# Holding one subtraction behind the last low part in the Fourier input folds of an encoder layer

## The chip, the cores and the metric

One core of a Trainium2 chip runs the whole layer as one program. The metric is the time of one execution on the device in microseconds (us). The five engines each take their own instructions in a fixed order: TensorE (PE: matmuls and transposes), VectorE (DVE), ScalarE (ACT), GpSimd (POOL) and SyncE (SP), which here issues nearly all transfers.

## The reference

The layer works on 256 tokens of width 2048 in float32. It is a feed-forward half-step, a pair of mixers, and a second feed-forward half-step. The change lies in the mixers:

```python
u = _rms_norm(h, pre_g)
q, k, v, f, g = jnp.split(u @ w_in, SPLIT_POINTS, axis=-1)
...
fg = f.astype(jnp.float32).reshape(b, s, FOURIER_GROUPS, FOURIER_GROUP_DIM)
mixed = jnp.real(jnp.fft.fft2(fg, axes=(1, 3), norm='ortho'))
...
gates = jax.nn.sigmoid((g.reshape(b, s, N_BRANCHES, D_MODEL) + b_gate).astype(jnp.float32)).astype(h.dtype)
merged = gates[:, :, 0] * y_attn + gates[:, :, 1] * y_four
```

The columns f (8 groups of 128 channels) go through a two-dimensional Fourier transform over tokens and over the channels of a group, of which the real part is kept. The columns q, k, v feed an attention, and g gives two gates.

## The kernel before, in words

**Split operands.** Every matmul operand is held as two float32r tiles, a high part and a low part: `split` (lines 101 and 102) lets ACT copy the source into the high part and then lets DVE subtract that from the source into the low part. A product is then three matmuls (`mm3`, lines 106 to 108): high by high, high by low, low by high. The function also remembers its last two instructions in `latest`; `latest["V"]` is the low part's subtraction on DVE.

**Weights.** A weight block of 512 columns and 2048 rows is walked by `col_block` in four groups `kg` of 512 rows. Each group comes in two pieces of 512 KB into `raw` tiles (5 buffers) and is split into `whi` and `wlo` tiles out of a ring of 6 slots. Each group costs PE 24 matmuls (4 row chunks, 2 token tiles, 3 products).

**Folds of f.** The weights of f are not multiplied as they are. The Fourier transform of real numbers has mirrored channels, so the host orders the columns of each of the 16 row chunks in pairs, and the kernel forms sums and differences of mirrored columns before it multiplies. For row chunk k, `load_f(k)` (line 615, with the helper `add_on_the_way` before it) issues a load of 512 KB from SP into a tile `fraw`, and then a second transfer from POOL's queue that adds the mirrored columns onto the front part on the way in, so that the front part holds sums (line 613). The tiles `fraw` live in the `chunk` pool, 6 slots in all (3 of each of two tags, used in turn), so the load of chunk k+6 takes the slot of chunk k.

`fold_f(k)` (line 622) then asks for the load of chunk k+4, and forms the differences in place on DVE (line 630: minus two times the back part, plus the sums). It splits the whole tile (`whi` on ACT, `wlo` on DVE), runs 12 matmuls into the two accumulators `pe`, and adds the sums, weighted by one scalar per row, into `zs` on DVE (line 643; line 641 for k = 0). That last instruction reads only the front part and one column pair behind it, which the subtraction doesn't write. The slot of `fraw` k is free when `wlo` of k, the last reader, is done.

**Where the folds stand.** Folds are called from inside four column blocks (the first block of q, and three of the gates) at row chunks 1, 5, 9 and 13, so one fold per group of weights: per fold the source has two raw pieces split, then one fold. Beside them lie the normalization and rotation of k and q (`norm_rope`, lines 535 to 558) and the gates (line 789).

**What sets the order.** The source order is not the order on the engines. A scheduler at build time orders each engine's instructions by when it thinks they are ready, within the dependencies it sees; on the chip each engine then keeps that order and waits at each instruction for what it needs. `tc.issue_after(ins)` adds an ordering without a wait: what is traced inside the block stands behind `ins` on `ins`'s engine. A stretch of DVE's order at the end of the first feed-forward step is written out by hand (`last_rows`), and instructions from outside may be put between its own.

Of the kernel before, what the change touches and what calls it, by code (L numbers as in the profile page):

```python
# [15 lines left out]
ALU = mybir.AluOpType  # L16
# [8 lines left out]
NB = 512  # L25
# [8 lines left out]
OW = GH * (HW - 1)  # L34
PO = 2 * (HW - 1)
NS = 2 * GH
EW = OW + NS
# [17 lines left out]
def encoder_layer(  # L55
# [23 lines left out]
    V, A, T = nc.vector, nc.scalar, nc.tensor  # L79
# [18 lines left out]
    latest = {}  # L98

    def split(hi, lo, src):  # L100
        a = A.activation(hi, src, AF.Copy)  # L101
        v = V.tensor_tensor(out=lo, in0=src, in1=hi.bitcast(F32), op=ALU.subtract)  # L102
        latest["A"], latest["V"] = a.ins, v.ins

    def mm3(ps, lh, ll, rh, rl, first, last):
        T.matmul(ps, lh, rh, start=first, stop=False)  # L106
        T.matmul(ps, lh, rl, start=False, stop=False)  # L107
        return T.matmul(ps, ll, rh, start=False, stop=last)  # L108
# [415 lines left out]
    for nm, g in (("q", gq), ("k", gk)):  # L524
        gc = const.tile([P, NT, HD], F32, name="gc" + nm)
        gs = const.tile([P, NT, HD], F32, name="gs" + nm)
        for t in range(NT):
            V.tensor_tensor(out=gc[:, t, :], in0=rc[:, t, :], in1=g[:], op=ALU.mult)
            v = lambda a: a.rearrange("p (a h c) -> p a h c", a=2, h=2)
            for half in range(2):  # L530
                V.tensor_tensor(out=v(gs[:, t, :])[:, :, half, :], in0=v(rsn[:, t, :])[:, :, half, :],
                                in1=v(g[:])[:, :, 1 - half, :], op=ALU.mult)
# [82 lines left out]
    def load_f(k):  # L615
        raw = chunk.tile([P, 2, NB], F32, tag=("ch_hi", "ch_lo")[k % 2], name="fraw")
        src = w_f[k].rearrange("p (b c) -> p b c", b=2)
        load(raw[:], src)
        add_on_the_way(raw[:, :, 0:OW], src[:, :, EW:NB])
        fraw[k] = raw  # L620

    def fold_f(k):

        if k == 0:
            pfold[0] = pmm.tile([P, NB], F32, tag="mm", name="pe")
            pfold[1] = ptr.tile([P, NB], F32, tag="tr", name="pe")
        if k + F_AHEAD < KD:
            load_f(k + F_AHEAD)
        raw = fraw.pop(k)
        V.scalar_tensor_tensor(out=raw[:, :, EW:NB], in0=raw[:, :, EW:NB], scalar=-2.0, in1=raw[:, :, 0:OW],  # L630
                               op0=ALU.mult, op1=ALU.add)
        hi = wring.tile([P, 2, NB], F32R, tag="hi", name="whi")
        lo = wring.tile([P, 2, NB], F32R, tag="lo", name="wlo")
        split(hi[:], lo[:], raw[:])
        e, o = slice(0, EW), slice(EW, NB)
        for b in range(2):
            mm = mm3(pfold[b][:, e], ueo[0][0][:, k, :], ueo[0][1][:, k, :], hi[:, b, e], lo[:, b, e], k == 0, False)
            with tc.issue_after(mm.ins):
                mm3(pfold[b][:, o], ueo[1][0][:, k, :], ueo[1][1][:, k, :], hi[:, b, o], lo[:, b, o], False, k == KD - 1)
        if k == 0:  # L640
            V.tensor_scalar(out=z2[:], in0=raw[:, :, e], scalar1=o0[:, k:k + 1], scalar2=None, op0=ALU.mult)
        else:
            V.scalar_tensor_tensor(out=z2[:], in0=raw[:, :, e], scalar=o0[:, k:k + 1], in1=z2[:],  # L643
                                   op0=ALU.mult, op1=ALU.add)
        if k == KD - 1:
            fs.extend(chunk.tile([P, 2, NB], F32R, tag="ch_" + c, name="f" + c[0]) for c in ("hi", "lo"))
            for b in range(2):
                split(fs[0][:, b, :], fs[1][:, b, :], pfold[b][:])
# [3 lines left out]
    def folds_at(n):  # L652

        now = [folds.pop(0) for _ in range(n)]
        return [(1 + i * KD // n, lambda k=k: fold_f(k)) for i, k in enumerate(now)]
# [389 lines left out]
```

## Time and profile before

| | us |
|---|---|
| median of 3 runs | 2133.01 (2130.24 to 2136.04) |
| the profiled execution, time | 2134.86 |
| its span in the profile | 2133.1 |
| PE busy | 2071.1 (97%) |
| DVE busy | 1317.3 (62%) |
| ACT busy | 1008.7 (47%) |
| POOL busy | 50.9 (2%) |

How to read it: the profiled execution's time is 1.8 us more than its span, and 1.9 us more than the median. A row of the waits says which engine and line waited for which, the total, the count and the longest. A row of a timeline begins with the start and the duration in us; a bracket at its end gives the idle time of the engine just before, and what ended it. SPq is SP issuing a transfer; the time to landing is not in that row. A row of the windows has the stretch and its length, the busy time and count of PE, PEld, DVE, ACT and POOL, the clock that PE was granted (1 is full), the DMA engines' share and GB/s. A row of a chain of waits has the start, the length and what the time was spent in.

### The profile page before, as it was taken

Reading aid. Unit: us, or ns where it says so; the run is one execution under the profiler, and the core shown is the slowest. Engines: PE = TensorE matmul, PEld = TensorE weight load, DVE = VectorE, ACT = ScalarE, POOL = GpSimd, SP = SyncE. Lnnn points to the kernel's source line nnn. Section 1 sums busy time; section 2 is a strip of 40 time slices with the busy share of each in tenths; the row PEclk is TensorE's granted clock in tenths of the full one; section 3 lists DMA queues with packets and bytes.
Section 4 is the critical chain, followed back from the end, with each engine's and each line's share of the span. In section 5 each row is a group of like instructions: output and inputs, shape, how many; then the busy total and the mean of one; then the engine's idle time right before and its main releaser. Section 6 shows DMA issues by size and latency. Waiting matters only on the chain.

```text
span 2133.1 us, 25216 instructions
## 1 busy us (share of the span) xinstructions
PE 2071.1 (97%) x9466; PEld 1713.9 (80%) x9466; DVE 1317.3 (62%) x1682; ACT 1008.7 (47%) x1336; POOL 50.9 (2%) x46
## 2 busy tenths in 40 slices
PE   9999999999999988779999999999999999999998
PEld 7888888888888867668888888878888888888886
DVE  6545555555555877546888887774455555555556
ACT  6444444444444546334676564554444444444443
POOL 0000000000000200000000000100000000000001
PEclk9999999999999999989999999999999999999999
DMA  8666555556566675554655657656555565555563
GB/s 316 209 219 191 190 189 192 193 190 191 186 194 195 211 241 174 159 157 134 194 183 188 198 174 246 209 170 207 195 189 190 186 197 193 191 189 188 192 194 108
DMA packets 117866, 411.10 MB, mean 193 GB/s; under 512 B 12872, under 2 KB 19024, under 8 KB 116336
## 3 DMA queue, kind: packets, MB, share of 16 engines
q1 hardware_dynamic: 113392, 405.36, 57.9%
q0 software_dynamic: 4352, 4.13, 1.3%
q8 instruction: 74, 1.21, 0.2%
q14 instruction: 48, 0.39, 0.0%
HBM read 405.25 MB, written 4.19 MB: 192 GB/s over the span
## 4 chain that ended last, share of the span: by engine, by line
PE 87%; DMA 6%; DVE 5%; issue 1%; ACT 1%; POOL 0%; SPq 0%; DVEq 0%; ACTq 0%; POOLq 0%
PE pc L107 17%; PE pc L108 17%; PE pc L106 17%; PE pr L108 10%; PE pr L107 10%; PE pr L106 10%; DMA fraw<-in_w_f 5%; DVE wlo L102 2%; PE pt L177 1%; DMA raw<-in_w_fo 1%; ACT whi L101 0%; DVE zs L643 0%; PE pt L760 0%; DVE h L390 0%; PE pf L108 0%
## 5 line engine op out<-in xcount | busy, mean ns | idle before, releaser
L102 DVE TENSOR_TENSOR wlo<-raw,whi 128x1024 fp32r<-128x1024 f32 (+1 forms) x711 | 866.8, 1222 | 672.1 <-ACT whi L101 670.6
L101 ACT ACTIVATE whi<-raw 128x1024 fp32r<-128x1024 f32 (+1 forms) x711 | 751.7, 1060 | 901.5 <-PE pc L108 534.9
L107 PE MATMUL pc<-wlo,uh 128*128 128x512 f32 x1840 | 720.9, 392 | 8.0 <-DVE wlo L102 8.0
L106 PE MATMUL pc<-whi,uh 128*128 128x512 f32 x1840 | 722.7, 393 | 5.5 <-ACT vt L846 3.4
L108 PE MATMUL pc<-whi,ul 128*128 128x512 f32 x1840 | 720.5, 392 | 1.9 <-DVE ul L102 1.9
L107 PEld LDWEIGHTS pc<-wlo,uh 128*128 128x128 f32 x1840 | 347.7, 189 | 81.0 <-DVE wlo L102 10.9
L106 PEld LDWEIGHTS pc<-whi,uh 128*128 128x128 f32 x1840 | 348.0, 189 | 78.1 <-ACT vt L846 3.8
L108 PEld LDWEIGHTS pc<-whi,ul 128*128 128x128 f32 x1840 | 347.8, 189 | 75.6 <-DVE ul L102 3.2
L106 PE MATMUL pr<-whi,hTh 128*128 128x512 f32 x688 | 269.4, 392 | 0.0
L108 PE MATMUL pr<-whi,hTl 128*128 128x512 f32 x688 | 267.8, 389 | 0.0
L107 PE MATMUL pr<-wlo,hTh 128*128 128x512 f32 x688 | 267.8, 389 | 0.0
L108 PEld LDWEIGHTS pr<-whi,hTl 128*128 128x128 f32 x688 | 129.1, 188 | 26.9
L107 PEld LDWEIGHTS pr<-wlo,hTh 128*128 128x128 f32 x688 | 129.2, 188 | 26.1
L106 PEld LDWEIGHTS pr<-whi,hTh 128*128 128x128 f32 x688 | 129.2, 188 | 26.1
L219 DVE TENSOR_TENSOR yf<-pr,yf 128x512 f32<-128x512 f32 (+1 forms) x82 | 55.1, 674 | 10.3 <-PE pr L108 9.7
L219 DVE TENSOR_TENSOR y<-pr,y 128x512 f32<-128x512 f32 x80 | 54.8, 686 | 4.1 <-PE pr L108 3.6
L106 PE MATMUL pr<-whi,oTh 128*128 128x512 f32 x128 | 50.3, 393 | 0.0
L108 PE MATMUL pr<-whi,oTl 128*128 128x512 f32 x128 | 50.0, 390 | 0.0
L107 PE MATMUL pr<-wlo,oTh 128*128 128x512 f32 x128 | 49.9, 390 | 0.0
L630 DVE SCALAR_TENSOR_TENSOR fraw<-fraw 128x504 f32<-128x504 f32 x16 | 10.9, 683 | 63.0 <-DMA fraw<-in_w_f 63.0
L106 PE MATMUL pr<-whi,mTh 128*128 128x512 f32 x120 | 46.9, 390 | 0.0
L108 PE MATMUL pr<-whi,mTl 128*128 128x512 f32 x120 | 46.7, 389 | 0.0
(300 smaller groups left out, 1416.7 us busy)
## 6 DMA issues: line engine op xcount, KB each, us to landing
raw<-in_f_up SPq DMA_DIRECT2D x176, 512.0 KB, 4.6
raw<-in_f_down SPq DMA_DIRECT2D x176, 512.0 KB, 4.5
raw<-in_f_gate SPq DMA_DIRECT2D x175, 512.0 KB, 4.3
raw<-in_w_in SPq DMA_DIRECT2D x112, 512.0 KB, 4.7
raw<-in_w_ao SPq DMA_DIRECT2D x32, 512.0 KB, 3.9
raw<-in_w_out SPq DMA_DIRECT2D x32, 512.0 KB, 4.5
fraw<-in_w_f SPq DMA_DIRECT2D x16, 512.0 KB, 4.5
raw<-in_w_fo SPq DMA_DIRECT2D x16, 512.0 KB, 4.4
```

What stands on the lines that cost most here:

```text
L101: a = A.activation(hi, src, AF.Copy)
L102: v = V.tensor_tensor(out=lo, in0=src, in1=hi.bitcast(F32), op=ALU.subtract)
L106: T.matmul(ps, lh, rh, start=first, stop=False)
L107: T.matmul(ps, lh, rl, start=False, stop=False)
L108: return T.matmul(ps, ll, rh, start=False, stop=last)
L177: T.transpose(pt[:, j, :], src[:, j * P:(j + 1) * P], ident[:])
L219: V.tensor_tensor(out=dst, in0=ps, in1=dst, op=ALU.add)
L630: V.scalar_tensor_tensor(out=raw[:, :, EW:NB], in0=raw[:, :, EW:NB], scalar=-2.0, in1=raw[:, :, 0:OW], op0=ALU.mult, op1=ALU.add)
```

## The change

The subtraction that forms the differences is put in a block that orders it behind `latest["V"]`, which at that place is the `wlo` of the second raw piece of the same group of weights. Nothing else in the source changes; the arithmetic is the same.

```diff
@@ fold_f(k)
         raw = fraw.pop(k)
-        V.scalar_tensor_tensor(out=raw[:, :, EW:NB], in0=raw[:, :, EW:NB], scalar=-2.0, in1=raw[:, :, 0:OW],
-                               op0=ALU.mult, op1=ALU.add)
+        with tc.issue_after(latest["V"]):
+            V.scalar_tensor_tensor(out=raw[:, :, EW:NB], in0=raw[:, :, EW:NB], scalar=-2.0, in1=raw[:, :, 0:OW],
+                                   op0=ALU.mult, op1=ALU.add)
         hi = wring.tile([P, 2, NB], F32R, tag="hi", name="whi")
         lo = wring.tile([P, 2, NB], F32R, tag="lo", name="wlo")
         split(hi[:], lo[:], raw[:])
```

In the changed file every line from 630 on stands one lower, so the subtraction is line 631 there and the accumulation of `zs` is line 644.

The first place is DVE at the end of the first feed-forward step, inside the stretch that is written by hand (`tot`, `pre`, `ca` to `cr` are steps of a root that scales the second token tile, `wlo<-raw` are low parts of weights, `fraw<-fraw` is the subtraction). Before:

```order
L376 TENSOR_REDUCE tot<-ssq_1997 128x1
L630 SCALAR_TENSOR_TENSOR fraw<-fraw 128x2x252
L378 TENSOR_SCALAR pre<-tot 128x1
L630 SCALAR_TENSOR_TENSOR fraw<-fraw 128x2x252
L156 SCALAR_TENSOR_TENSOR ca<-ssq_1997,pre 128x1
L630 SCALAR_TENSOR_TENSOR fraw<-fraw 128x2x252
L157 TENSOR_SCALAR ci<-ca 128x1
L102 TENSOR_TENSOR wlo<-raw,whi 128x1024
```

And with the change:

```order
L376 TENSOR_REDUCE tot<-ssq_1997 128x1
L378 TENSOR_SCALAR pre<-tot 128x1
L156 SCALAR_TENSOR_TENSOR ca<-ssq_1997,pre 128x1
L157 TENSOR_SCALAR ci<-ca 128x1
L102 TENSOR_TENSOR wlo<-raw,whi 128x1024
```

The subtractions of chunks 0 to 2 have left this stretch. Those of chunks 3, 4 and 5, which stood between low parts of weights in the block after it, have left that too; all six now stand among the folds.

The second place is DVE in the folds of the second column block, from the low part of chunk 2 to that of chunk 4 (`wlo<-fraw` is a fold's low part; `zs<-fraw` is the accumulation). Before, in the first two rows of `fraw<-fraw` and `zs` the chunk is 8, in the next two 9:

```order
L102 TENSOR_TENSOR wlo<-raw,whi 128x1024 x2
L630 SCALAR_TENSOR_TENSOR fraw<-fraw 128x2x252
L643 SCALAR_TENSOR_TENSOR zs<-fraw,o_5824,zs 128x520
L102 TENSOR_TENSOR wlo<-fraw,whi 128x1024
L102 TENSOR_TENSOR wlo<-raw,whi 128x1024 x2
L630 SCALAR_TENSOR_TENSOR fraw<-fraw 128x2x252
L643 SCALAR_TENSOR_TENSOR zs<-fraw,o_5824,zs 128x520
L102 TENSOR_TENSOR wlo<-fraw,whi 128x1024
```

With the change the rows of `fraw<-fraw` are chunks 2, 3 and 4, and those of `zs` chunks 7, 8 and 9:

```order
L631 SCALAR_TENSOR_TENSOR fraw<-fraw 128x2x252
L644 SCALAR_TENSOR_TENSOR zs<-fraw,o_5824,zs 128x520
L102 TENSOR_TENSOR wlo<-fraw,whi 128x1024
L102 TENSOR_TENSOR wlo<-raw,whi 128x1024 x2
L631 SCALAR_TENSOR_TENSOR fraw<-fraw 128x2x252
L102 TENSOR_TENSOR wlo<-fraw,whi 128x1024
L644 SCALAR_TENSOR_TENSOR zs<-fraw,o_5824,zs 128x520
L102 TENSOR_TENSOR wlo<-raw,whi 128x1024 x2
L631 SCALAR_TENSOR_TENSOR fraw<-fraw 128x2x252
L644 SCALAR_TENSOR_TENSOR zs<-fraw,o_5824,zs 128x520
L102 TENSOR_TENSOR wlo<-fraw,whi 128x1024
```

Before, the subtraction and the accumulation of one chunk stand together, and the low part behind them is that of a chunk five lower. Now the subtraction is that of the very chunk whose low part follows, and the accumulation has stayed where it was, five chunks ahead; it isn't ordered by the change. Counted over the folds, the accumulation of chunk k+5 stands ahead of the low part of chunk k for k = 1, 2, 4, 5, 6, 7, 9 and 10, and behind it for k = 3 and 8; before, the subtraction of chunk k+5 stood ahead of it for k = 1, 3, 4, 5, 6, 8, 9 and 10, and behind it for k = 2 and 7. SP's loads of chunks 6 to 15 keep their places between the pieces of weights, and POOL's order is the same.

## The prediction

> **What bounds the kernel now.** I read the page first, then PE's waits, the windows around them, the chain of waits there, and at last the rows of DVE.
>
> ```profile
> PE 2071.1 (97%) x9466; PEld 1713.9 (80%) x9466; DVE 1317.3 (62%) x1682; ACT 1008.7 (47%) x1336; POOL 50.9 (2%) x46
> L630 DVE SCALAR_TENSOR_TENSOR fraw<-fraw 128x504 f32<-128x504 f32 x16 | 10.9, 683 | 63.0 <-DMA fraw<-in_w_f 63.0
> PE pe L107 <- DVE wlo L102: 26.0, 8, 7.3
> PE pc L107 <- DVE wlo L102: 8.0, 5, 6.2
> PE pe L106 <- ACT q L546: 6.2, 1, 6.2
> PE pc L106 <- ACT vt L846: 3.4, 1, 3.4
> 820.00:860.00 40.00, 32.13 (x155) 26.88 (x154) 24.68 (x45) 18.51 (x31) 3.27 (x3) 0.91 0.57 159
> 957.40:964.30 6.90, 6.90 (x38) 5.93 (x37) 3.68 (x3) 4.25 (x6) 0.00 (x0) 1.00 0.57 178
> ```
>
> PE is busy for all but 62 us, and 44 of these are the four waits above. Behind them is DVE: the subtraction sits idle for 63 us in front of transfers into `fraw`. The folds run far below PE's pace: from 820 to 860 PE is busy 32 of 40 us at a clock of 0.91, while a window after the last subtraction is full, at a clock of 1. The chain of waits shows one turn of the folds, and DVE's rows (last two for SP) give ten such turns and their extremes:
>
> ```profile
> 858.59 3.53 DMA fraw<-in_w_f
> 862.79 5.15 DMA fraw<-in_w_f
> 868.63 0.76 DVE zs L643
> 869.38 1.15 DVE wlo L102
> 870.54 4.14 DMA fraw<-in_w_f
> 819.74 1.22 DVE L102 TENSOR_TENSOR wlo<-fraw,whi 128x1024 fp32r<-128x1024 f32 x1
> 833.21 1.22 DVE L102 TENSOR_TENSOR wlo<-fraw,whi 128x1024 fp32r<-128x1024 f32 x1
> 842.86 1.23 DVE L102 TENSOR_TENSOR wlo<-fraw,whi 128x1024 fp32r<-128x1024 f32 x1 [0.48 <-ACT whi L101]
> 868.03 0.69 DVE L630 SCALAR_TENSOR_TENSOR fraw<-fraw 128x504 f32<-128x504 f32 x1 [7.19 <-DMA fraw<-in_w_f]
> 870.43 2.35 DVE L102 TENSOR_TENSOR wlo<-raw,whi 128x1024 fp32r<-128x1024 f32 x2
> 891.10 1.22 DVE L102 TENSOR_TENSOR wlo<-fraw,whi 128x1024 fp32r<-128x1024 f32 x1
> 900.21 1.22 DVE L102 TENSOR_TENSOR wlo<-fraw,whi 128x1024 fp32r<-128x1024 f32 x1
> 939.27 1.22 DVE L102 TENSOR_TENSOR wlo<-fraw,whi 128x1024 fp32r<-128x1024 f32 x1
> 957.52 1.23 DVE L102 TENSOR_TENSOR wlo<-fraw,whi 128x1024 fp32r<-128x1024 f32 x1 [0.17 <-ACT whi L101]
> 964.39 1.23 DVE L102 TENSOR_TENSOR wlo<-fraw,whi 128x1024 fp32r<-128x1024 f32 x1 [1.50 <-ACT whi L101]
> 844.11 0.33 SPq L82 DMA_DIRECT2D fraw<-in_w_f  x1
> 856.07 0.68 DVE L630 SCALAR_TENSOR_TENSOR fraw<-fraw 128x504 f32<-128x504 f32 x1 [7.25 <-DMA fraw<-in_w_f]
> 882.35 0.33 SPq L82 DMA_DIRECT2D fraw<-in_w_f  x1
> 890.50 0.68 DVE L630 SCALAR_TENSOR_TENSOR fraw<-fraw 128x504 f32<-128x504 f32 x1 [0.47 <-DMA fraw<-in_w_f]
> ```
>
> The loop closes on itself. The low part of chunk k frees the slot, at once SP loads chunk k+6 into it (858.59), POOL adds the mirrored columns (862.79), and 9.4 us after the load the subtraction of k+6 starts (868.03). On DVE this subtraction stands ahead of the low part of chunk k+1 (869.30). DVE asks for a transfer and stands still until it has landed, with the next fold's low part, which PE needs, behind it. Ten turns, from the first `wlo<-fraw` at 819.74 to the eleventh at 939.27, take 119.5 us. Two of them were short, 9.65 (833.21 to 842.86) and 9.11 (891.10 to 900.21), where the order has the low part ahead of the subtraction; the other eight average (119.5 - 18.8) / 8 = 12.6. Without a wait a turn is PE's: 964.39 - 957.52 = 6.87.
>
> **The change, part by part.** The subtraction is moved; nothing is added or removed, no transfer changes its place on SP between weights or on POOL. What counts is what now stands first in front of a transfer. The accumulation `zs` reads the same sums, so it needs both transfers of its chunk, and in the new order `zs` of chunk k+5 stands where the pair stood, ahead of the low part of chunk k. So the wait is not gone: it passes from line 630 to line 644, and the slot is still freed by the last low part. I cost three parts.
>
> *First, the folds.* A full turn before was transfer, subtraction, `zs`, low part: 12.6 = transfer + 0.60 (868.03 to 868.63) + 0.67 (to 869.30) + 1.2, so about 10.1 to 10.2 for the transfer; the extremes are 844.11 to 856.07, 11.96, and 882.35 to 890.50, 8.15. Now the subtraction is that of chunk k+1 and needs no transfer; it runs before the wait, and so does the high part that ACT makes from it. A full turn becomes 10.2 + 0.67 + 1.2 = 12.1, and 12.2 with the one or two small root steps that the order puts between `zs` and the low part. Eight turns remain full. The two short ones are now those into chunks 3 and 8, where no root or rotation lies between: two raw low parts 2.35, subtraction 0.68, the high part 1.06, the low part 1.22, together 5.3. PE's pace of 6.87 is the bound only later, since the full turn behind starts its load at the low part, not at PE's matmul. Eight times 12.2 and two times 5.3 are 108.2 against 119.5: 11 us saved. From both sides: if the short turns take 9.4 as before, 116.4 and a gain of 3; at most 8 times 11.5 and two of 5.3, a gain of 17.
>
> ```profile
> 864.35 1.06 ACT L101 ACTIVATE whi<-fraw 128x1024 fp32r<-128x1024 f32 x1
> 747.39 0.68 DVE L630 SCALAR_TENSOR_TENSOR fraw<-fraw 128x504 f32<-128x504 f32 x1 [1.41 <-DMA fraw<-in_w_f]
> 752.67 0.68 DVE L630 SCALAR_TENSOR_TENSOR fraw<-fraw 128x504 f32<-128x504 f32 x1 [3.86 <-DMA fraw<-in_w_f]
> 753.33 1.22 DVE L102 TENSOR_TENSOR wlo<-raw,whi 128x1024 fp32r<-128x1024 f32 x1
> 754.60 0.80 PE L107 MATMUL pc<-wlo,uh 128*128 128x512 f32 x1 [6.21 <-DVE wlo L102]
> 753.15 0.42 ACT L101 ACTIVATE dps<-draw 128x258 fp32r<-128x258 f32 x1 [6.52 <-DMA draw<-in_dft_pos]
> 759.08 1.21 DVE L102 TENSOR_TENSOR wlo<-raw,whi 128x1024 fp32r<-128x1024 f32 x1
> 795.39 0.68 DVE L630 SCALAR_TENSOR_TENSOR fraw<-fraw 128x504 f32<-128x504 f32 x1 [7.49 <-DMA fraw<-in_w_f]
> 799.58 0.17 ACT L579 ACTIVATE o<-pt 128x4 f32<-128x4 f32 x1 [6.24 <-DVE uol L102]
> 801.35 0.50 PE L106 MATMUL pc<-whi,uh 128*128 128x512 f32 x1 [3.40 <-ACT vt L846]
> ```
>
> *Second, the end of the first feed-forward step.* Chunks 0 to 2 were subtracted in the hand-written stretch, at 747.39 to 753.27, with idle times of 1.41 and 3.86, and the low part behind them (753.33) let PE wait 6.21. These go: the low part at 753.33 comes some 6.7 us earlier. The low part at 759.08 comes earlier by that and by the five instructions on loaded tables that have left the stretch between, about 8 in all. PE doesn't keep all of it: its next transposition needs a product that now stands behind the first instruction on those tables, and their transfers were on the way at that time; ACT's wait for a constant issued just behind them ended only at 753.15. The trace doesn't show when the tables landed. I take 5, nearer to the 6.21 than to nothing; the bounds are 2 (they land as late as that constant, and PE waits for most of the time) and 8.
>
> *Third, chunk 5.* Its subtraction idled 7.49 (795.39); behind it ACT waited 6.24 (799.58) and PE 3.40 (801.35). Now only `zs` of chunks 0 to 5 remains there, whose transfers landed long before. PE's 3.4 becomes about half a us: gain 3, bounds 2 and 4.
>
> After the loop, subtractions 11 to 15 run in turns at PE's pace, where DVE is busy 3.68 of 6.90; 0.68 more is free under PE. If that cover were gone, it would be 5 times 0.68, 3.4 us. In the loop the wait for the transfer hides the subtraction.
>
> Sum: 11 + 5 + 3 = 19. The profiled execution took 2134.86, so 2115.9; it lies 1.85 above the median of 2133.01, on whose scale the forecast is **2114 us**. By the parts' bounds alone the gain is 7 to 29.
>
> **The rivals.**
>
> *The wait goes altogether* (what one would expect from the words of the change). All folds then run at 6.87:
>
> ```profile
> 836.84 0.59 PE L106 MATMUL pe<-whi,ueh 128*128 128x260 f32 x1 [6.24 <-ACT q L546]
> 940.55 0.58 PE L107 MATMUL pe<-wlo,ueh 128*128 128x260 f32 x1 [2.84 <-DVE wlo L102]
> ```
>
> Ten turns of PE from 836.84 would end at 905.5 instead of 940.55, 35 us, and PE's 6.2 in front of it and the 8 of parts two and three come on top: 49 us, 2084. Against it: `zs` waits for the same two transfers, at the same place of the order.
>
> *The transfers get quicker*, for whatever cause; for the same bytes the trace has 8.15 to 11.96. With 8.15 a full turn is 10.1: 8 × 10.1 + 10.6 = 91.4, a gain of 28 + 8 = 36, 2097. The Trainium skill, page "DMA: Bandwidth & Descriptors", section "Anatomy of one DMA — SWDGE (gpsimd) path", fits a transfer as 2 us and its bytes over 436 GB/s. By that the two transfers, 512 and 252 KB, would take 3.2 and 2.6 us, 5.8 together, an estimate by that page; the turn would then be 7.7, little above PE's own, and the time close to the first rival's 2084. The ten transfers of this trace, 8.15 at the least, don't agree with it.
>
> *The wait stays and the short turns are lost.* If a slot of the ring or ACT holds up the high part, all ten turns are full: 122 against 119.5. Then parts two and three stand alone against a loss of 2.5: 5.5 us, 2127.5.
>
> *Slower: the high part comes late.* Before, a chunk was subtracted long before its high part was due. Now ACT must wait for DVE, and DVE then for ACT. If the subtraction ended up behind the wait instead of ahead of it, each turn would carry 0.68 and 1.06 more: 10 × 13.9 = 139, 19.5 more than now, less 8: 2144.5. It decides from the point at which the slot for the high part comes free later than the landing. Against it: line 631 stands ahead of line 644 in the order, and ACT's high part at 864.35 was through 2.6 us before the wait ended at 868.03.
>
> *The change does nothing*, if the subtraction stood there already: 2133. The order says it moved.
>
> **How the numbers follow.** Forecast 0.66; the wait goes 0.07; quicker transfers 0.07; short turns lost 0.13; slower 0.05; nothing 0.02. What can be told from no change is about 0.3%, 6.4 us. The forecast's own range is 2106 to 2124. For eight in ten I go on to the quicker transfers on one side and to the lost short turns on the other: 2098 to 2128. Faster gets the forecast, the first two rivals and a little of the third, 0.82; no difference the rest of the third, the last, and a little of the forecast, 0.12; slower 0.06.
>
> **What would show it.** Right: line 631's idle time falls from 63.0 to almost nothing, and line 644, which had none, has 30 to 45 us for transfers into `fraw`; `wlo<-fraw` from the first to the eleventh takes some 108 us, with two turns under 8; PE's waits for `wlo` at the folds shrink but stay above 15; the 6.21 and 3.40 are gone or below 4 together with what takes their place. Wrong: if line 644 hardly waits and turns are near 7, the wait was freed elsewhere; if line 631 waits or ACT idles for it inside turns, the high part is late; if turns are near 10 with the wait in place, the transfers became quicker.

## The result, and the profile after

| | before | with the change |
|---|---|---|
| median, us | 2131.62 (2128.19 to 2136.04) | 2111.72 (2110.32 to 2112.66) |
| ratio to before, 95% interval | | 0.9905 (0.9885 to 0.9925) |
| the profiled execution, time | 2134.86 | 2111.38 |
| its span in the profile | 2133.1 | 2109.6 |

The change makes the kernel about 20 us faster, between the forecast of 2114 and the lower end of its own range, 2106. The runs of before here were taken beside the changed kernel and have a median 1.4 below the one shown earlier.

The page of the changed kernel begins its busy times like this, and these are the waits of PE and of DVE's line 644 that bear on the change (engine and line, what it waited for, us in total, times, longest):

```profile
PE 2065.4 (98%) x9466; PEld 1711.0 (81%) x9466; DVE 1317.7 (62%) x1682; ACT 1008.5 (48%) x1336; POOL 50.8 (2%) x46
PE pe L107 <- DVE wlo L102: 16.0, 6, 6.1
PE pe L106 <- ACT q L546: 6.3, 1, 6.3
PE pc L107 <- DVE wlo L102: 2.0, 2, 1.0
PE pt L177 <- DVE y L404: 1.7, 3, 1.0
PE pe L106 <- ACT whi L101: 1.6, 2, 1.2
DVE zs L644 <- DMA fraw<-in_w_f: 36.4, 7, 7.1
```

Line 631, the subtraction, no longer waits for any transfer. Before, its idle time was 63.0. Line 644, the accumulation `zs`, had no such wait and now has 36.4. One more idle time, of 4.22 ahead of `zs` at 852.18, is put to no releaser in the profile ("issue"); POOL's transfer into that tile was issued at 845.75, 6.4 earlier, which is the median time to landing of these transfers, so it very likely belongs with them and makes eight waits:

```profile
852.18 0.76 DVE L644 SCALAR_TENSOR_TENSOR zs<-fraw,o,zs 128x520 f32<-128x520 f32 x1 [4.22 <-issue]
```

PE's waits for `wlo` at the folds (`pe`) went from 26.0 to 16.0, its 6.2 in front of a `pc` product went, its 3.4 for ACT's `vt` went, and the wait for `q` stayed (6.2 before, 6.3 now).

The folds themselves, from DVE's rows of the changed kernel. A bracket gives the idle time just before and what ended it:

```profile
806.10 0.68 DVE L631 SCALAR_TENSOR_TENSOR fraw<-fraw 128x504 f32<-128x504 f32 x1
807.95 1.22 DVE L102 TENSOR_TENSOR wlo<-fraw,whi 128x1024 fp32r<-128x1024 f32 x1
814.19 0.68 DVE L631 SCALAR_TENSOR_TENSOR fraw<-fraw 128x504 f32<-128x504 f32 x1
820.49 0.76 DVE L644 SCALAR_TENSOR_TENSOR zs<-fraw,o,zs 128x520 f32<-128x520 f32 x1 [4.56 <-DMA fraw<-in_w_f]
821.24 1.22 DVE L102 TENSOR_TENSOR wlo<-fraw,whi 128x1024 fp32r<-128x1024 f32 x1
...
856.27 0.68 DVE L631 SCALAR_TENSOR_TENSOR fraw<-fraw 128x504 f32<-128x504 f32 x1
864.03 0.76 DVE L644 SCALAR_TENSOR_TENSOR zs<-fraw,o,zs 128x520 f32<-128x520 f32 x1 [7.09 <-DMA fraw<-in_w_f]
864.71 1.22 DVE L102 TENSOR_TENSOR wlo<-fraw,whi 128x1024 fp32r<-128x1024 f32 x1
...
918.37 0.76 DVE L644 SCALAR_TENSOR_TENSOR zs<-fraw,o,zs 128x520 f32<-128x520 f32 x1 [6.25 <-DMA fraw<-in_w_f]
919.04 1.22 DVE L102 TENSOR_TENSOR wlo<-fraw,whi 128x1024 fp32r<-128x1024 f32 x1
```

The subtraction runs early and free (814.19, 856.27). Then DVE stands at `zs` of a chunk five higher, and the low part that PE needs comes right behind it. SP's queue shows that the loop is still closed. The low part at 807.95 ends at 809.17, and the load into the slot that it freed is issued at 809.21, which with POOL's accumulation behind it is what `zs` at 820.49 waits for (rows of SP and of POOL):

```profile
809.21 0.33 SPq L82 DMA_DIRECT2D fraw<-in_w_f  x1
814.06 1.08 POOL L613 DMA_DIRECT2D fraw<-in_w_f  x1 [27.11 <-DMA fraw<-in_w_f]
```

Where the 20 us come from. The two executions already stand apart ahead of the change: the same product, behind the same wait for `ul`, starts at 744.24 before (first row) and at 741.93 after (second row). The subtractions that moved stood behind that point, and the run below that leaves chunks 0 to 5 as before has this product at 742.15; so these 2.3 us are no effect of the change and are taken off below.

```profile
744.24 0.50 PE L108 MATMUL pc<-whi,ul 128*128 128x512 f32 x1 [1.16 <-DVE ul L102]
```

```profile
741.93 0.51 PE L108 MATMUL pc<-whi,ul 128*128 128x512 f32 x1 [1.03 <-DVE ul L102]
```

| stretch, by the low parts of the folds | before | after | gain |
|---|---|---|---|
| first `wlo<-fraw`, net of 2.3 | 819.74 | 807.95 | 9.5 |
| ten turns, first to eleventh | 119.53 | 111.09 | 8.4 |
| five turns behind them | 32.00 | 29.52 | 2.5 |

Together 20.4, and the span less the same 2.3 lost 21.2. The medians differ by 19.9, so of these figures, which come from one execution of each kernel, about a microsecond is the executions' own. The ten turns after were 13.29, 12.36, 5.25, 14.01, 11.85, 10.62, 13.93, 5.25, 13.52 and 11.01.

### The profile page after: what moved, and what is told of

Same layout as the page of the kernel before. It is cut to its first block, busy times and chain, and to the rows that moved or that the text cites. A ratio compares the mean times of both kernels' runs of the same rounds, so it can differ in the third digit from the quotient of the medians.

```text
span 2109.6 us, 25216 instructions
## 1 busy us (share of the span) xinstructions
PE 2065.4 (98%) x9466; PEld 1711.0 (81%) x9466; DVE 1317.7 (62%) x1682; ACT 1008.5 (48%) x1336; POOL 50.8 (2%) x46
## 4 chain that ended last, share of the span: by engine, by line
PE 53%; DVE 3%; DMA 2%; issue 1%; ACT 0%; DVEq 0%; POOLq 0%; ACTq 0%
PE pc L106 10%; PE pc L108 10%; PE pc L107 10%; PE pr L108 6%; PE pr L107 6%; PE pr L106 6%; DMA fraw<-in_w_f 1%; DVE wlo L102 1%; PE pt L177 1%; DMA raw<-in_w_fo 1%; PE pt L761 0%; PE pf L108 0%; PE pf L106 0%; PE pf L107 0%; DVE h L390 0%
## 5 line engine op out<-in xcount | busy, mean ns | idle before, releaser
L107 PE MATMUL pr<-wlo,mTh 128*128 128x512 f32 x120 | 46.7, 389 | 0.0
```

## The experiments

All times below are compared with runs of the kernel before on the same chip (medians 2132.05 for the first four and 2131.15 for the last four). Where a table of turns says "first", it is the start of the first `wlo<-fraw`, net of how far the execution stood from the profile of before ahead of the change, by the row quoted at 744.24 and its like (1.7 to 2.2 us).

### Both consumers held

The theory is that the wait was handed from the subtraction to `zs`, and that this wait, through the slot that the low part behind it frees, closes the loop. So `zs` is held as well, from chunk 1 on; `latest["V"]` is at that place the fold's own low part:

```diff
         else:
-            V.scalar_tensor_tensor(out=z2[:], in0=raw[:, :, e], scalar=o0[:, k:k + 1], in1=z2[:],
-                                   op0=ALU.mult, op1=ALU.add)
+            with tc.issue_after(latest["V"]):
+                V.scalar_tensor_tensor(out=z2[:], in0=raw[:, :, e], scalar=o0[:, k:k + 1], in1=z2[:],
+                                       op0=ALU.mult, op1=ALU.add)
```

> The accumulation zs (from chunk 1 on) is held behind the low part of its own chunk too, so that nothing that needs a transfer stands ahead of an older low part on DVE. Theory (the wait was passed from the subtraction to zs, and this wait, with the slot that the low part behind it frees, closes the loop): the wait of zs for fraw, 36.4 us in the changed kernel, falls below 3; the turns from low part to low part go to PE's pace, about 7 instead of 11.1; PE's waits for wlo at the folds (16.0) and for q (6.3) go, and some lowered clock: 2111.7 - 27 = about 2085. Rival (what holds the folds is the ring of weights, ACT's high part or PE itself, and zs only idles beside it): turns stay above 10 and the time within 4 us of 2111.7.

Measured: 2077.73 us, ratio 0.9748 (0.9733 to 0.9763). `zs` has no wait for a transfer left. The ten turns take 75.5 us, down from 111.1. The busy times and PE's wait for `q`, then one turn of DVE, then a window in the middle of the folds (length, busy time and count of PE, PEld, DVE, ACT and POOL, granted clock, DMA share, GB/s) and the loads' median landing:

```profile
PE 2054.5 (99%) x9466; PEld 1702.2 (82%) x9466; DVE 1317.6 (63%) x1682; ACT 1008.3 (49%) x1336; POOL 50.9 (2%) x46
PE pe L106 <- ACT q L546: 1.2, 1, 1.2
832.89 1.22 DVE L102 TENSOR_TENSOR wlo<-fraw,whi 128x1024 fp32r<-128x1024 f32 x1 [1.18 <-ACT whi L101]
834.04 0.75 DVE L645 SCALAR_TENSOR_TENSOR zs<-fraw,o,zs 128x520 f32<-128x520 f32 x1
834.71 2.35 DVE L102 TENSOR_TENSOR wlo<-raw,whi 128x1024 fp32r<-128x1024 f32 x2
836.98 0.67 DVE L631 SCALAR_TENSOR_TENSOR fraw<-fraw 128x504 f32<-128x504 f32 x1
838.83 1.23 DVE L102 TENSOR_TENSOR wlo<-fraw,whi 128x1024 fp32r<-128x1024 f32 x1 [1.18 <-ACT whi L101]
820.00:860.00 40.00, 40.00 (x215) 34.48 (x214) 34.36 (x60) 24.29 (x44) 5.47 (x5) 1.00 0.87 242
fraw<-in_w_f SPq DMA_DIRECT2D x16, 512.0 KB, 6.5
```

PE is busy for all of 820 to 860, at a full clock; in the changed kernel it was so for 32.17 of these 40 us, at 0.87:

```profile
820.00:860.00 40.00, 32.17 (x153) 27.50 (x154) 23.10 (x31) 17.19 (x27) 4.12 (x4) 0.87 0.62 175
```

DVE still waits 1.18 in eight of the ten turns, for its own high part on ACT, and PE is kept busy all the same. The transfers were not made quicker (the load's median landing is 6.5 us here); they are only no longer waited for. The theory's 2085 was 7 too high, because the waits that went took lowered clock with them. PE's busy time for the same 9466 matmuls is 10.9 below that of the changed kernel, and its idle time 23 below (2109.6 - 2065.4 = 44.2 and 2075.7 - 2054.5 = 21.2). Even the wait for `q` fell, from 6.3 to 1.2. Steps of the root on which `q` rests stand on DVE behind the `zs` that waits at 820.49 in the changed kernel.

### Only zs held

```diff
-        with tc.issue_after(latest["V"]):
-            V.scalar_tensor_tensor(out=raw[:, :, EW:NB], ...)
+        V.scalar_tensor_tensor(out=raw[:, :, EW:NB], ...)
...
+            with tc.issue_after(latest["V"]):
+                V.scalar_tensor_tensor(out=z2[:], ...)
```

> From the kernel before, with zs alone held behind the low part of its own chunk; the subtraction is free again. Theory (either consumer, standing early, keeps the loop closed): the subtraction waits for fraw 50 to 65 us as before and the turns stay at 11.5 to 12.6 (zs, 0.67, has left the turn): 2126 to 2132. Rival (zs is the one that matters, the subtraction's wait is harmless): about as fast as with both held, below 2100.

Measured: 2132.69 us, ratio 1.0003 (0.9994 to 1.0012); ten turns take 122.4. DVE's waits and two of its rows:

```profile
DVE fraw L631 <- DMA fraw<-in_w_f: 69.7, 14, 8.5
852.90 0.68 DVE L631 SCALAR_TENSOR_TENSOR fraw<-fraw 128x504 f32<-128x504 f32 x1 [7.00 <-DMA fraw<-in_w_f]
853.50 1.22 DVE L102 TENSOR_TENSOR wlo<-fraw,whi 128x1024 fp32r<-128x1024 f32 x1
```

The wait is at the subtraction, as before, with the low part right behind it. With this run the four combinations are complete: neither held 2132, the subtraction alone 2112, `zs` alone 2133, both 2078. What counts is that *no* instruction that needs the new transfer stands ahead of the low part that must come first. The idle time, 69.7, and the time came out a little above what was expected; the turns, 12.2 on average, lie within it, but the 0.67 of `zs` that left the turn did not shorten them.

### The subtraction held for some chunks only

Four runs hold the subtraction for some chunks and leave it free, as before, for the others. The edit of the changed kernel, here for chunks 0 to 5:

```diff
-        with tc.issue_after(latest["V"]):
+        with (tc.issue_after(latest["V"]) if k < 6 else ExitStack()):
```

> The subtraction is held for chunks 0 to 5 alone, those that stood in the end of the first feed-forward step and in the block behind it; chunks 6 to 15 as before. Theory (the parts add up): the gain of parts two and three alone, 9.5 us by the shift of the first low part of a fold between the two traces: 2131.6 - 9.5 = 2122, and the loop's ten turns 116 to 120. Rival (what is gained ahead of the loop is lost in it, since the loop waits for transfers anyway): 2129 or more.

> The subtraction is held for chunks 6 to 15 alone; chunks 0 to 5 as before. Theory (the parts add up): the gain in the loop, 8.4, and what came behind it, 2.8: 2131.6 - 11 = 2120.5; the wait of 6.21 for a low part near 754 and the 7.5 of the subtraction of chunk 5 are there again. Rival (the loop's gain comes from its earlier start only, its turns being as long as before): within 3 us of 2131.6.

> From the kernel before, the subtraction held for chunks 0 to 2 alone (part two by itself: the waits of 1.41 and 3.86 in the hand-written stretch at the end of the first feed-forward step go). Theory: the third low part of the next block came 6.6 us earlier net of the offset of the two traces, and PE keeps most of it: 2132 - 6 = 2126; the 7.5 in front of the subtraction of chunk 5 stays. Rival: PE waits for the tables instead, and less than 2.5 us is gained: 2129.5 or more.

> From the kernel before, the subtraction held for chunks 3 to 5 alone (part three by itself: the 7.49 in front of the subtraction of chunk 5 goes). Theory: PE's wait of 3.4 for ACT goes and nothing else: 2132 - 3 = 2129, and with the run before this one 9 to 9.5, the 10 us that holding chunks 0 to 5 gained. Rival: nothing is gained, since the loop starts earlier but waits for its transfers all the same: 2131 or more.

| held for | time, us | ratio (95% interval) | first, net gain | ten turns | five behind |
|---|---|---|---|---|---|
| none (before) | 2132.05, 2131.15 | | 0 | 119.5 | 32.0 |
| 0 to 5 | 2122.05 | 0.9954 (0.9941 to 0.9966) | 9.2 | 120.1 | 31.7 |
| 6 to 15 | 2123.97 | 0.9963 (0.9951 to 0.9976) | 0 | 114.0 | 29.5 |
| 0 to 2 | 2129.85 | 0.9993 (0.9982 to 1.0003) | -0.4 | 117.1 | 29.2 |
| 3 to 5 | 2130.10 | 0.9997 (0.9989 to 1.0006) | 5.0 | 122.5 | 30.8 |
| all | 2111.72 | 0.9905 (0.9885 to 0.9925) | 9.5 | 111.1 | 29.5 |

The first two agree with the theory that they add up: 10.0 and 8.1 us against the medians are 18.1, where the whole change gained 20. The loop alone fell 3 short of its 11: its ten turns were 114.0, not 111.1, and behind the loop it gained 2.5 where 2.8 was expected.

The last two contradict theirs. Chunks 0 to 2 and 3 to 5 were to bring 6 and 3, and by their intervals each brought something between a loss of 1.3 and a gain of 3.8, yet together 10. For chunks 0 to 2 the profile shows where the gain went ahead of the folds. PE's and DVE's rows, first around the end of the first feed-forward step and then around chunk 5:

```profile
748.67 0.50 PE L107 MATMUL pc<-wlo,uh 128*128 128x512 f32 x1 [1.03 <-DVE wlo L102]
793.20 0.68 DVE L631 SCALAR_TENSOR_TENSOR fraw<-fraw 128x504 f32<-128x504 f32 x1 [7.89 <-DMA fraw<-in_w_f]
798.03 0.80 PE L106 MATMUL pc<-whi,uh 128*128 128x512 f32 x1 [7.32 <-ACT vt L847]
```

PE's 6.21 is gone (748.67, with 1.03 left). But the subtraction of chunk 5, which stands early here as before, starts at 793.20, that is 2.2 earlier than before (795.39), and this execution stood 2.1 earlier anyway. The transfers of chunk 5 had not come forward with PE. SP issued the load at 780.98 here and at 781.63 before, and POOL its accumulation at 788.62 here and at 787.41 before; why SP comes to it no earlier stays open. PE came to the wait for `vt` at 798.03 - 7.32 = 790.71, where before it came at 801.35 - 3.40 = 797.95. That is 7.2 earlier, 5.1 net. It then stood there 7.32 instead of 3.40. So part two earns its 5 us, and a wait whose end has not moved takes 3.9 of them back before the folds begin. Behind that point the account stays open: the row of this run in the table adds up to a gain of 4.8 (-0.4, 2.4 and 2.8), where the medians give 1.3. Its folds have an order of their own, and how much of their 5.2 belongs to that order and how much to this one execution isn't shown.

For chunks 3 to 5 the low parts start 5.0 earlier net, but the ten turns are 2.9 longer, and the order inside them is not that of before either. PE's wait for `q` grew to 7.5, and one turn took 17.3, where before none was over 14.5. Which of these costs what was not separated.

### The transfer made shorter

The changed kernel without POOL's accumulating transfer, so that it leaves out the sums of mirrored columns:

```diff
         load(raw[:], src)
-        add_on_the_way(raw[:, :, 0:OW], src[:, :, EW:NB])
         fraw[k] = raw
```

> The changed kernel without POOL's accumulating transfer (the mirrored columns are then not added, so the result is not the layer's); the order keeps zs of chunk k+5 ahead of the low part of chunk k, now in all ten turns. Theory (the length of the transfer sets the turn): a turn is the load alone, 4.5 to 6.5 by the medians of the landings, 0.67 and 1.2, so 6.5 to 8.6 and near PE's pace; ten turns 65 to 86 instead of 111.1, and the time 2078 to 2092. Rival (the turn is set by something else that goes with the order, such as the ring or ACT): ten turns above 105, and the time above 2105.

Measured: 2085.05 us, ratio 0.9787 (0.9771 to 0.9802). DVE's first and eleventh low part, and SP's loads (median us to landing in the last column):

```profile
806.73 1.23 DVE L102 TENSOR_TENSOR wlo<-fraw,whi 128x1024 fp32r<-128x1024 f32 x1
891.89 1.22 DVE L102 TENSOR_TENSOR wlo<-fraw,whi 128x1024 fp32r<-128x1024 f32 x1
fraw<-in_w_f SPq DMA_DIRECT2D x16, 512.0 KB, 5.1
```

Ten turns take 85.2, 8.5 each, the upper end of what was expected, though `zs` stands ahead of the older low part in all ten of them. So in the changed kernel it is the length of the two transfers that makes the turns 11.1; the ring of weights and ACT's high part are the same in this run and don't. Here `zs` waits for a transfer in six places only, 13.1 us in all. The time is still above that of holding both, where the two transfers are there and nothing waits for them.

### zs held from chunk 6 on

```diff
-            with tc.issue_after(latest["V"]):
+            with (tc.issue_after(latest["V"]) if k >= 6 else ExitStack()):
                 V.scalar_tensor_tensor(out=z2[:], ...)
```

> As the run with both held, but zs is held from chunk 6 on alone; zs of chunks 0 to 5 stands early again, where its transfers have landed long before. Theory (only what stands early in front of a transfer still on its way costs anything): the same time as with both held, 2078 within 3 us. Rival (zs of chunks 0 to 5 costs DVE time that the end of the first block needs, or there is more DVE work in the folds otherwise): 4 us or more apart.

Measured: 2077.27 us, ratio 0.9750 (0.9737 to 0.9764), the same as with both held. So an instruction that stood early, where its transfer had landed, cost nothing that these runs can tell. The version to keep is either of the two.

## Why the prediction was right, point by point

- **The mechanism.** The prediction said that the wait passes from line 630 to line 644 instead of going away, with 30 to 45 us there. It measured 36.4 (40.6 with the wait at 852.18), and the run with both held shows that this wait, with the lowered clock that went with it, was worth another 34 us (2111.72 to 2077.73). The rival by which it goes altogether was put at 2084, and that is nearly what the kernel with both held takes.
- **The loop, 11 us by the sum, 8.4 measured.** The two short turns were foreseen at 5.3 and took 5.25, in the two places named. The full turns were foreseen at 12.2, and the eight average (111.09 - 10.50) / 8 = 12.57, about what they took before (12.6). The mis-sized term is the transfer: 10.2 was carried over from before, while in the changed kernel it takes 10.7 from the load to `zs`, as the mean of the eight that DVE stood waiting for (9.1 to 12.1). The median landing of SP's loads of `fraw` rose from 4.5 to 6.0 us (first row before, second after):

```profile
fraw<-in_w_f SPq DMA_DIRECT2D x16, 512.0 KB, 4.5
```

```profile
fraw<-in_w_f SPq DMA_DIRECT2D x16, 512.0 KB, 6.0
```

  The DMA engines' share between 820 and 860 rose too, from 0.57 to 0.62. That the two belong together is likely but was not tested.
- **Parts two and three, 8 us by the sum, 9.5 measured**, 10 with chunks 0 to 5 alone. The 6.21 became 1.01 and the 3.40 went. The tables, the open price of part two, cost DVE a single wait of 0.30:

```profile
748.46 0.50 PE L107 MATMUL pc<-wlo,uh 128*128 128x512 f32 x1 [1.01 <-DVE wlo L102]
749.37 0.29 DVE L528 TENSOR_TENSOR gcq<-rc,gq 128x128 f32<-128x128 f32 x1 [0.30 <-DMA rc<-in_rope_cos]
```

  So 5 was the right size for part two on PE (5.1 net where it was alone). The sum, however, treated parts two and three as independent, and they are not: each by itself moves the time by about a microsecond. The prediction didn't see that part two's gain has to pass the wait of part three, where the run with chunks 0 to 2 lost 3.9 of it.
- **Behind the loop, nothing by the sum, 2.5 measured.** The prediction took these turns for PE's alone in both kernels. Before, the last stall of the loop, 2.84 at 940.55, was followed by matmuls at a lowered clock; after, the last stall is 1.80 and no such matmul follows. The windows of 10 us behind the two stalls, before (first) and after (second), say so:

```profile
940.55:950.55 10.00, 10.00 (x39) 8.54 (x40) 7.00 (x7) 3.72 (x4) 0.00 (x0) 0.69 0.61 181
```

```profile
920.31:930.31 10.00, 10.00 (x57) 8.67 (x58) 8.25 (x10) 4.68 (x6) 0.00 (x0) 1.00 0.49 157
```

  Whether a stall of this size lowers the clock isn't settled by its length (last section). That the change is the cause of these 2.5 is therefore not shown.
- **The sum.** 19 foreseen, 20 measured: a loop that gave 2.6 less, and 1.5 and 2.5 more ahead of it and behind it. That these nearly cancel is luck; the mechanism and each of the three parts came out within their bounds without it. The high part on ACT was not late. PE's waits for `whi` at the folds are 1.6 in all.
- **The transfer's price by the Trainium skill.** The Trainium skill's page "DMA: Bandwidth & Descriptors", section "Anatomy of one DMA — SWDGE (gpsimd) path", has the fit of 2 us and the bytes over 436 GB/s, by which both transfers would take 5.8 us, an estimate. It is for transfers issued by GpSimd, and here only the second is one. The changed kernel took 9.1 at the least from the load to `zs` where DVE waited, and the load of 512 KB alone 5.1 in the run without the accumulation, against 3.2 by that fit. The measurements decide against it here, as the prediction took it.

## What to carry to other kernels

Where an engine that takes its work in order stands idle in front of a transfer, moving the one instruction that waits hands the wait to the next consumer of the same transfer; list all of them, and look for each at what is queued behind it, above all at whatever frees the buffer that the next transfer needs. In this kernel holding one consumer gave 20 us or nothing, and holding both gave 54. And a gain ahead of a wait whose end is set by a transfer can be lost in that wait: here the two parts gave about a microsecond each alone, and 10 together.

## What the runs showed of the hardware

Removing stalls gave more than the stalls' own length. PE's busy time for the same 9466 matmuls fell from 2071.1 before to 2054.5 with both held; these 16.6 us are in no row of waits. They go with the granted clock, as the rows behind a stall show. The first four rows here follow the stall of 2.84 at 940.55, the next two are the same shapes 8 us later in the same execution, and the last is the second product behind the stall of 3.40 at 801.35:

```profile
941.15 0.41 PE L106 MATMUL pe<-whi,uoh 128*128 128x252 f32 x1
941.36 0.42 PE L107 MATMUL pe<-wlo,uoh 128*128 128x252 f32 x1
943.08 0.63 PE L106 MATMUL pc<-whi,uh 128*128 128x512 f32 x1
943.51 0.63 PE L107 MATMUL pc<-wlo,uh 128*128 128x512 f32 x1
...
949.57 0.39 PE L107 MATMUL pc<-wlo,uh 128*128 128x512 f32 x1
951.05 0.28 PE L106 MATMUL pe<-whi,uoh 128*128 128x252 f32 x1
```

```profile
801.69 0.39 PE L107 MATMUL pc<-wlo,uh 128*128 128x512 f32 x1
```

Behind the 2.84 the folds' products took 0.42 instead of 0.28, at steps of 0.21 instead of 0.12, and eight products of 512 columns took 0.63 instead of 0.39, at steps of 0.43 instead of 0.23. Eleven times 0.1 and eight times 0.2 are 2.7 us, as much as the stall itself, and close to the 2.5 that came free behind the loop. Behind the longer stall of 3.40 nothing ran slow. Two other runs differ in the same way. The first two rows here are from the run with chunks 0 to 2 held, where nothing ran slow behind 2.76; the last three are from the run with chunks 0 to 5 held, where two stalls of 1.44 and 1.37 with one product between them were followed by the same eleven and eight slow products:

```profile
936.45 0.39 PE L107 MATMUL pe<-wlo,ueh 128*128 128x260 f32 x1 [2.76 <-DVE wlo L102]
936.79 0.28 PE L106 MATMUL pe<-whi,uoh 128*128 128x252 f32 x1
...
855.61 0.39 PE L106 MATMUL pe<-whi,ueh 128*128 128x260 f32 x1 [1.44 <-ACT whi L101]
857.37 0.58 PE L107 MATMUL pe<-wlo,ueh 128*128 128x260 f32 x1 [1.37 <-DVE wlo L102]
859.90 0.63 PE L106 MATMUL pc<-whi,uh 128*128 128x512 f32 x1
```

So a stall cost its length alone in some rows and nearly twice its length in others, and which of the two can't be read from its length.

The Trainium skill's page "TensorE: Matmul & The Clock Gate", section "Part 1: The HAM clock gate (the "warmup" mystery)", describes a window of about 3.4 us that runs on freely, and half the clock after an idle one. Steps nearly twice as long agree with half the clock, and a stall of 3.40 without any slowing fits a window that is not tied to the stall. That 2.84 was enough to slow PE, or 1.44 and 1.37 with a product between, is less than a whole idle window and goes beyond what the page says.
